# Layer 1's gating products traced ahead of the state-space mixer's last input product, and norms without GpSimd, in a two-layer hybrid block

## The chip, the cores and the metric

The kernel runs on one core of a Trainium2 chip. The metric is the device time of one execution in microseconds (us), the median of three runs. The engines are TensorE (PE, matmuls; PEld is its weight load), VectorE (DVE), ScalarE (ACT), GpSimd (POOL) and SyncE (SP, which issues the DMAs here). The granted clock of a row is TensorE's, as a share of 2.4 GHz; its lower level is 1.2 GHz.

## The reference, cut to what matters

Two layers over 512 latent tokens and 256 context tokens, width 1024. Each layer is: norm and modulation, one input projection for four mixers, output projection, norm and gated residual; then norm and modulation, gated feed-forward, norm and gated residual.

```python
def rmsnorm(x, g):
    return x * lax.rsqrt(jnp.mean(x * x, axis=-1, keepdims=True) + EPS) * g
for l in range(DEPTH):
    hx = rmsnorm(x, g_pre_mix[l]) * (1.0 + sc1x) + sh1x        # hc: the same of ctx
    in_x = jnp.split(hx @ w_in[l], SPLITS, axis=-1)             # four mixers' columns
    oa_x = chunk_mlp(in_x[0], ...)          # A: gelu; u * (spatial gate of v)
    ob_c, ob_x = gla_mixer(in_c[1], in_x[1], ...)   # B: gated linear attention
    oc_c, oc_x = s5_mixer(in_c[2], in_x[2], ...)    # C: state-space scan, both directions
    od_c, od_x = mla_mixer(in_c[3], in_x[3], ...)   # D: latent attention
    mix_x = jnp.concatenate([oa_x, ob_x, oc_x, od_x], axis=-1) @ w_out[l]
    x = x + gt1x * rmsnorm(mix_x, g_post_mix[l])
    hx = rmsnorm(x, g_pre_ffn[l]) * (1.0 + sc2x) + sh2x
    x = x + gt2x * rmsnorm(conv_ffn(hx, ...), g_post_ffn[l])
    if l < DEPTH - 1: ...                    # the same for ctx
return x
```

## The kernel before

Features lie on partitions and tokens along the free dimension. The tokens are three groups of 256: groups 0 and 1 are the latent tokens, group 2 is the context. Every fp32 weight is split into a high part (ACT, L191, `whi`) and a low part (DVE, L192, `wlo`), and so is every normed activation (`hh`/`hl`, for groups 0 and 1 together `hhx`/`hlx`); a product is three matmuls (L199 to L201) for each of eight blocks of the contraction. All DMAs go through SP's queue. The order of the instructions on each engine is chosen by the language's scheduler, which takes the order of the program text as priority; each engine then works through its own list in order. The program text is arranged by hand: the layers follow one another, and in the feed-forward `weave` mixes products ("units") with the steps of the norms ("chains") by scripts.

A norm of a group has a post-norm and, before a mixer or a feed-forward, a pre-norm. `sums` squares on ACT (L308), adds on DVE (L311) and sums over partitions on PE (L322); `rstd` takes the power on GpSimd (L125) and spreads it over the partitions on PE (L145), in PSUM. `post_norm` multiplies y by it and by the gate, and adds to x (L415 to L420). `modulate` scales and shifts x and splits it (L384 to L391). Of the eight blocks of 128 features, five go over DVE with the PSUM operand and three over GpSimd, which takes a copy in SBUF (L339).

At the boundary of the layers, group 0's, 1's and 2's post-norms and modulations follow one another. Mixer C's input products of layer 1 (`c_units`, ACT's copy L1218 into `rawm`) are units of layer 0's feed-forward, group after group; the last two, of group 2, come when group 2 is modulated. Then `mixers` opens its own PSUM pools and traces:

- `mixer_c`: transposes of `rawm` (L686), copies, second transposes (L693), B-products (L704), copies into the state `s5v` on DVE and ACT (L712, L714), then the scan on DVE: seven wide steps and eleven narrow ones (L725 to L728), and its wide closing passes (L743 to L753). The state is copied to `s5a` (L764, L766), multiplied out (L776, L778), goes through a gelu (L782), is transposed back (L788) and multiplied by the GLU's weights (L804 to L808), and is stored to `dmixr`.
- the other input products, in PSUM tiles `pg`: mixer A's u (`ua`, two products of 24 matmuls of 128x512) and v (`va`, 96 of 128x256, tokens on partitions), and mixer A (L980 to L995); then B's gates (products L835; ACT L838 to L842; DVE's subtraction L845, scan L846, L848 to L850), D's queries and keys and their norms (L1029 to L1044), B's q and k (L864, L869).

## Time and profile before

| | before |
|---|---|
| median of 3 runs | 1911.69 us (1909.13 to 1919.33) |
| the profiled execution | 1913.68 us |
| its span, from first to last instruction | 1911.9 us |
| mean granted clock of TensorE | 0.943 |

The span and what lies around it (1.8 us) make the profiled execution's time. All durations of the trace come from that one execution.

### The profile page before, as it was taken

Reading aid. Unit: us, or ns where it says so; the run is one execution under the profiler, and the core shown is the slowest. Engines: PE = TensorE matmul, PEld = TensorE weight load, DVE = VectorE, ACT = ScalarE, POOL = GpSimd, SP = SyncE. Lnnn points to the kernel's source line nnn. Section 1 sums busy time; section 2 is a strip of 40 time slices with the busy share of each in tenths; the row PEclk is TensorE's granted clock in tenths of the full one; section 3 lists DMA queues with packets and bytes.
Section 4 is the critical chain, followed back from the end, with each engine's and each line's share of the span. In section 5 each row is a group of like instructions: output and inputs, shape, how many; then the busy total and the mean of one; then the engine's idle time right before and its main releaser. Section 6 shows DMA issues by size and latency. Waiting matters only on the chain.

```text
span 1911.9 us, 28200 instructions
## 1 busy us (share of the span) xinstructions
PE 1778.6 (93%) x11256; PEld 1515.5 (79%) x11256; DVE 1197.0 (63%) x2200; ACT 775.5 (41%) x1241; POOL 122.3 (6%) x142
## 2 busy tenths in 40 slices
PE   5899989899988899999999998997989999999997
PEld 2785777689967788888888887886768988888886
DVE  8866634654899754684774674683465665454545
ACT  3433454444653333332331344364344653333332
POOL 0000000000430000000000033000000320000002
PEclk7999998899999999999999987998789899999998
DMA  9457630005623343352443333322102623323241
GB/s 351 154 174 243 192 95 23 28 26 201 199 66 120 113 133 99 114 163 78 148 128 111 101 120 104 113 70 86 43 23 84 195 86 81 109 86 110 79 150 47
DMA packets 94386, 222.14 MB, mean 116 GB/s; under 512 B 10928, under 2 KB 41008, under 8 KB 93232
## 3 DMA queue, kind: packets, MB, share of 16 engines
q1 hardware_dynamic: 94256, 220.36, 37.1%
q8 instruction: 88, 1.44, 0.3%
q14 instruction: 42, 0.34, 0.1%
HBM read 193.35 MB, written 24.08 MB: 114 GB/s over the span
## 4 chain that ended last, share of the span: by engine, by line
PE 71%; DVE 12%; issue 9%; ACT 4%; DMA 2%; POOL 1%; SPq 1%; POOLq 0%; DVEq 0%; ACTq 0%
PE pf L199 16%; PE pf L200 16%; PE pf L201 16%; PE pg L199 3%; PE pg L201 3%; PE pg L200 3%; PE pb L243 1%; PE pd L1151 1%; DVE z L1205 1%; DVE wlo L192 1%; PE pn L322 1%; DVE nu L389 1%; DVE hlx L391 1%; PE pc L704 1%; DVE junk L236 1%
## 5 line engine op out<-in xcount | busy, mean ns | idle before, releaser
L192 DVE TENSOR_TENSOR wlo<-raw,whi 128x1024 fp32r<-128x1024 f32 (+1 forms) x215 | 252.4, 1174 | 306.2 <-ACT whi L191 303.4
L191 ACT ACTIVATE whi<-raw 128x1024 fp32r<-128x1024 f32 (+1 forms) x215 | 217.4, 1011 | 407.7 <-PE pf L200 346.4
L199 PE MATMUL pf<-hhx,whi 128*128 128x512 f32 (+1 forms) x1032 | 365.4, 360 | 13.8 <-DVE z L1205 4.8
L200 PE MATMUL pf<-hlx,whi 128*128 128x512 f32 (+1 forms) x1032 | 370.1, 360 | 5.6 <-DVE hlx L391 5.1
L201 PE MATMUL pf<-hhx,wlo 128*128 128x512 f32 (+1 forms) x1032 | 367.2, 357 | 0.3 <-DVE wlo L192 0.3
L199 PEld LDWEIGHTS pf<-hhx,whi 128*128 128x128 f32 x1032 | 200.1, 197 | 42.2 <-ACT hhx L390 6.2
L200 PEld LDWEIGHTS pf<-hlx,whi 128*128 128x128 f32 x1032 | 202.4, 196 | 34.0 <-DVE hlx L391 9.2
L201 PEld LDWEIGHTS pf<-hhx,wlo 128*128 128x128 f32 x1032 | 202.6, 196 | 26.1 <-DVE wlo L192 0.5
L199 PE MATMUL pf<-g,whi 128*128 128x512 f32 (+1 forms) x552 | 185.2, 341 | 5.4 <-DVE z L1205 2.8
L201 PE MATMUL pf<-g,wlo 128*128 128x512 f32 (+1 forms) x552 | 186.5, 340 | 0.8 <-DVE wlo L192 0.8
L200 PE MATMUL pf<-g,whi 128*128 128x512 f32 (+1 forms) x552 | 186.9, 340 | 0.0
L1205 DVE SCALAR_TENSOR_TENSOR z<-pf,cols,z 128x511 f32<-128x511 f32 (+1 forms) x264 | 168.0, 656 | 24.3 <-ACT z L1203 21.7
L200 PE MATMUL pf<-hl,whi 128*128 128x256 f32 x432 | 123.7, 287 | 1.4 <-DVE hl L391 1.4
L199 PE MATMUL pf<-hh,whi 128*128 128x256 f32 x432 | 121.6, 286 | 1.8 <-ACT hh L390 1.8
L201 PE MATMUL pf<-hh,wlo 128*128 128x256 f32 x432 | 122.9, 285 | 0.0
L199 PEld LDWEIGHTS pf<-g,whi 128*128 128x128 f32 x552 | 104.3, 191 | 19.3 <-issue 4.0
L201 PEld LDWEIGHTS pf<-g,wlo 128*128 128x128 f32 x552 | 105.3, 191 | 12.3 <-DVE wlo L192 1.0
L200 PEld LDWEIGHTS pf<-g,whi 128*128 128x128 f32 x552 | 105.2, 191 | 11.5 <-DVE g L1255 0.2
L1203 ACT ACTIVATE z<-pf,cols 128x512 f32<-128x512 f32 (+1 forms) x132 | 89.9, 694 | 34.5 <-PE pf L201 29.3
L1284 DVE TENSOR_TENSOR y<-y,pf 128x512 f32<-128x512 f32 (+1 forms) x88 | 44.2, 514 | 71.0 <-PE pf L201 70.7
L125 POOL TENSOR_TENSOR nroy<-nroy,mhalf 128x2 f32<-128x2 f32 x10 | 9.9, 994 | 1202.3 <-DVE nroy L124 894.8
L200 PEld LDWEIGHTS pf<-hl,whi 128*128 128x128 f32 x432 | 83.5, 193 | 3.8 <-DVE hl L391 2.2
(457 smaller groups left out, 3406.3 us busy)
## 6 DMA issues: line engine op xcount, KB each, us to landing
raw<-in_w SPq DMA_DIRECT2D x170, 512.0 KB, 3.6
rawm<-in_wmod SPq DMA_DIRECT2D x64, 512.0 KB, 4.1
raw<-in_w SPq DMA_DIRECT2D x48, 384.0 KB, 3.2
wm<-in_wmod SPq DMA_DIRECT2D x8, 1024.0 KB, 10.6
silu<-in_wmod SPq DMA_DIRECT2D x16, 512.0 KB, 5.4
dx<-g SPq DMA_DIRECT2D x32, 256.0 KB, 2.2
dG<-gt SPq DMA_DIRECT2D x16, 256.0 KB, 2.3
dE<-es SPq DMA_DIRECT2D x16, 256.0 KB, 2.6
```

Source lines behind the costliest of these rows:

```text
L191: nc.scalar.activation(hv, src, AF.Copy)
L192: nc.vector.tensor_tensor(lv, src, hv.bitcast(F32), op=ALU.subtract)
L199: self.nc.tensor.matmul(out, lh, rh, start=i == 0, stop=False)
L200: self.nc.tensor.matmul(out, lh, rl, start=False, stop=False)
L201: self.nc.tensor.matmul(out, ll, rh, start=False, stop=i == n - 1)
L236: self.nc.vector.scalar_tensor_tensor(junk[:], wt, 1.0, self.silu[w][:], op0=ALU.mult, op1=ALU.mult, accum_out=self.modacc[l][:, w, m:m + 1])
L243: self.nc.tensor.matmul(acc[32 * q:32 * q + 2, :], self.ct[:, k, :], halves[q // 2][:, q % 2 * 512:q % 2 * 512 + 512], start=k == 0, stop= ...
L322: self.nc.tensor.matmul(ps[:, j:j + 1], acc[:, k, j * 128:(j + 1) * 128], self.ones[:, 0:1], start=k == 0, stop=k == 1)
L389: nc.vector.scalar_tensor_tensor(u[:], xk, sc, pb, op0=ALU.mult, op1=ALU.mult)
L1203: nc.scalar.activation(z[:, o:o + m], p[:, :m], AF.Identity, bias=b, scale=w1)
L1205: self.last = nc.vector.scalar_tensor_tensor(z[:, o + d:o + d + m - 1], p[:, s:s + m - 1], w, z[:, o + d:o + d + m - 1], op0=ALU.mult, op1 ...
L1284: nc.vector.tensor_tensor(y[:, m, t0:t0 + tw], y[:, m, t0:t0 + tw], ps[:, :tw], op=ALU.add)
```

## The change

Two things are changed.

First, the units of group 2's input product of mixer C are no longer issued at the end of the feed-forward. Its PSUM pool stays open, and in layer 1 `mixers` traces in its banks (tag "pf") first va's product, then ua's, then the two late units; only then is the pool closed and are the mixers' pools opened. Since the late units come from a second call of `c_units`, their two weight halves are loaded and split a second time. In layer 0 mixer C is traced first as before; ua and va have changed places.

Second, GpSimd keeps only the power in the norms. After the squares ACT multiplies y by the gate in place; `post_norm` is then two DVE passes of 128x512 for each pair of blocks. `modulate` is, for each pair, one DVE product of 128x512, four ACT passes of 128x256 (scale and shift, once for the high part and once in full), and one DVE subtraction of 128x512.

```diff
@@ -333,16 +331,13 @@
     def feature_rstd(self, pool, psp, ptag, width, pv):
         return self.rstd(pool, self.sums(pool, psp, ptag, width, pv))
-    def pool_copy(self, pool, pb, x=""):
-
-        sb = self.t(pool, [128, 256], "npb" + x, bufs=1)
-        self.nc.scalar.copy(sb[:], pb)
-        return sb[:]
-
     def norms(self, l, part, g, yp, xp, pool, psp, store=None, pre=None):
         ps = self.sums(pool, psp, "pn", 512, yp, "o")
+        for k in range(KT):
+            yk = yp(k // 2)[:, k % 2, :]
+            self.nc.scalar.activation(yk, yk, AF.Copy, scale=self.modc(l, part, k, g))
         yield
         pb = self.rstd(pool, ps, "o")
         yield
@@ -370,26 +365,19 @@
             for _ in c:
                 pass
-    def modulate(self, l, part, g, pv, pool, pb, kdve=KDVE):
+    def modulate(self, l, part, g, pv, pool, pb):
         nc = self.nc
         self.new_h(g)
-        sb = self.pool_copy(pool, pb) if kdve < KT else None
-        for k in KORDER:
-            xk = pv(k // 2)[:, k % 2, :]
-            u = self.t(pool, [128, 256], "nu", bufs=3)
-            sh, sc = self.modc(l, part, k, g), self.modc(l, part + 1, k, g)
-            hh, hl = self.hh[g][:, k, :], self.hl[g][:, k, :]
-            if k >= kdve:
-                w = self.t(pool, [128, 256], "nw", bufs=2)
-                nc.gpsimd.tensor_tensor(u[:], xk, sb, op=ALU.mult)
-                nc.scalar.activation(hh, u[:], AF.Identity, bias=sh, scale=sc)
-                nc.scalar.activation(w[:], u[:], AF.Identity, bias=sh, scale=sc)
-                nc.gpsimd.tensor_tensor(hl, w[:], hh.bitcast(F32), op=ALU.subtract)
-            else:
-                nc.vector.scalar_tensor_tensor(u[:], xk, sc, pb, op0=ALU.mult, op1=ALU.mult)
-                nc.scalar.activation(hh, u[:], AF.Identity, bias=sh)
-                self.hlast = nc.vector.scalar_tensor_tensor(hl, u[:], sh, hh.bitcast(F32), op0=ALU.add,
-                                                            op1=ALU.subtract)
+        for i in range(KT // 2):
+            u = self.t(pool, [128, 2, 256], "nu", bufs=2)
+            nc.vector.tensor_tensor(u[:], pv(i), pb.unsqueeze(1).to_broadcast([128, 2, 256]), op=ALU.mult)
+            ks = slice(2 * i, 2 * i + 2)
+            w = self.t(pool, [128, 2, 256], "nw", bufs=2)
+            for k in (2 * i, 2 * i + 1):
+                sh, sc = self.modc(l, part, k, g), self.modc(l, part + 1, k, g)
+                nc.scalar.activation(self.hh[g][:, k, :], u[:, k % 2], AF.Identity, bias=sh, scale=sc)
+                nc.scalar.activation(w[:, k % 2], u[:, k % 2], AF.Identity, bias=sh, scale=sc)
+            self.hlast = nc.vector.tensor_tensor(self.hl[g][:, ks], w[:], self.hh[g][:, ks].bitcast(F32), op=ALU.subtract)
     def new_hx(self):
@@ -404,23 +392,14 @@
     def post_norm(self, l, part, g, yp, xp, pool, pb, squares):
-        acc, seen = None, set()
+        acc = None
         nc = self.nc
-        sb = self.pool_copy(pool, pb, "o")
-        for k in KORDER:
-            yk, xk = yp(k // 2)[:, k % 2, :], xp(k // 2)[:, k % 2, :]
-            u = self.t(pool, [128, 256], "nuo", bufs=2)
-            gate = self.modc(l, part, k, g)
-            if k >= KDVE:
-                nc.gpsimd.tensor_tensor(u[:], yk, sb, op=ALU.mult)
-                nc.scalar.activation(u[:], u[:], AF.Copy, scale=gate)
-                nc.gpsimd.tensor_tensor(xk, xk, u[:], op=ALU.add)
-            else:
-                nc.vector.scalar_tensor_tensor(u[:], yk, gate, pb, op0=ALU.mult, op1=ALU.mult)
-                nc.vector.tensor_tensor(xk, xk, u[:], op=ALU.add)
-            seen.add(k)
-            if squares and k ^ 1 in seen:
-                acc = self.square(pool, acc, xp(k // 2))
+        for i in range(KT // 2):
+            y, x = yp(i), xp(i)
+            nc.vector.tensor_tensor(y, y, pb.unsqueeze(1).to_broadcast([128, 2, 256]), op=ALU.mult)
+            nc.vector.tensor_tensor(x, x, y, op=ALU.add)
+            if squares:
+                acc = self.square(pool, acc, x)
         return acc
@@ -1379,8 +1358,13 @@
             ctx = l < L - 1
             G = (0, 1, 2) if ctx else (0, 1)
             tn = T if ctx else NX
-            self.mixers(l, ctx, md, (psls, tabs, tables) if l == 0 else None)
-            with self.pool("f") as fp, self.pool("psf", space=PSUM) as psp:
+            if l == 0:
+                self.mixers(l, ctx, md, early=(psls, tabs, tables))
+            else:
+                self.mixers(l, ctx, md, late=(psf, psp, late))
+            psf = self.pool("psf", space=PSUM)
+            psp = psf.__enter__()
+            with self.pool("f") as fp:
                 with self.pool("y1") as yp:
                     y = self.t(yp, [128, KT, T], "y")
                     def out_units(groups):
@@ -1488,17 +1472,18 @@
                     if ctx:
                         uf = [self.t(self.wp, [128, D], "rawm", bufs=2)[:, :T] for _ in range(2)]
                         self.uf[l + 1] = uf
-                        cu, late = self.c_units(l + 1, uf, psp)
+                        cu = self.c_units(l + 1, uf, psp)[0]
+                        late = self.c_units(l + 1, uf, psp)[1]
                         self.weave(WV[4], down[1], c[:1])
                         self.weave(WV[5], down[2] + cu[:2], c[:2])
                         self.weave(WV[6], cu[2:], c[1:])
-                        self.weave("", late, [])
                     else:
                         self.weave(WV[7], down[1], c)
             xsrc = xd
+        psf.__exit__(None, None, None)
         es.close()
-    def mixers(self, l, ctx, md, early=None):
+    def mixers(self, l, ctx, md, early=None, late=None):
         nc = self.nc
         G = (0, 1, 2) if ctx else (0, 1)
         G3 = (0, 1, 2)
@@ -1541,16 +1526,46 @@
         def store(o, k, mix, t0=0):
             nc.sync.dma_start(md[:, o + k, t0:tn], mix[:, t0:tn])
+        rest = iter(())
+
+        def visit(n):
+            for _ in range(n):
+                next(rest, None)
+
+        mxs = self.pool("mx")
+        px_ = mxs.__enter__()
+        env = SimpleNamespace()
+        x12 = self.t(px_, [128, 4, T], "x12")
+        x6 = self.t(px_, [128, 1536], "x6")
+        ut = x12[:, 0:2]
+        va = x12[:, 2:4].rearrange("p a t -> p (a t)").rearrange("p (i c) -> p i c", i=6)
+
+        def va_product():
+            tmajor("va", G, lambda g, ps: nc.scalar.activation(
+                va[:, 2 * g:2 * g + 2].rearrange("p i c -> p (i c)"), ps[:], AF.Gelu_apprx_tanh))
+
+        def ua_product():
+            for i in range(2):
+                px, pc = fm(half("ua", i), G)
+                evac(ut[:, i], px, pc, func=AF.Gelu_apprx_tanh)
+                visit(1)
+
+        if late:
+
+            psf, psp, units = late
+            self.psg = psp, "pf"
+            va_product()
+            ua_product()
+            for u in units:
+                u()
+            psf.__exit__(None, None, None)
         psls, tabs, tables = early or (self.pool("psb", space=PSUM), None, None)
         if not early:
             self.psp = psls.__enter__()
         pcs = self.pool("pcp", space=PSUM, side="right")
         pcp = pcs.__enter__()
         psgs = self.pool("psg", space=PSUM)
-        self.psg = psgs.__enter__()
-        mxs = self.pool("mx")
-        px_ = mxs.__enter__()
-        env = SimpleNamespace()
+        self.psg = psgs.__enter__(), "pg"
         def heads(n, x, groups):
             w = 256 * len(groups)
@@ -1575,16 +1584,9 @@
             if l == 0:
                 rest = chain(*(self.mod_pair(p, self.gate) for p in (1, 2)))
             visit(2)
-            x12 = self.t(px_, [128, 4, T], "x12")
-            x6 = self.t(px_, [128, 1536], "x6")
-            ut = x12[:, 0:2]
-            va = x12[:, 2:4].rearrange("p a t -> p (a t)").rearrange("p (i c) -> p i c", i=6)
-            for i in range(2):
-                px, pc = fm(half("ua", i), G)
-                evac(ut[:, i], px, pc, func=AF.Gelu_apprx_tanh)
-                visit(1)
-            tmajor("va", G, lambda g, ps: nc.scalar.activation(
-                va[:, 2 * g:2 * g + 2].rearrange("p i c -> p (i c)"), ps[:], AF.Gelu_apprx_tanh))
+            if not late:
+                ua_product()
+                va_product()
             visit(2)
             self.mixer_a(l, ut, va, x6, px_, "pb2", ctx)
             visit(2)
```

What the scheduler makes of it on PE, at the boundary. The names: `pf` and `pg` are products, `pn` norm sums (L322, now L320) and broadcast (L145, now L143), `pc` mixer C's tiles. Before: the end of group 2's product, the first transposes, ua's two products (pg_11117, pg_11149), va's first (pg_11187), the first B-product.

```order
L200 MATMUL pf_10698<-hl_1561_10631,whi_10433 128x256
...
L201 MATMUL pf_10698<-hh_1560_10630,wlo_10434 128x256
L686 MATMUL pc_1585_10774<-cst_68,rawm_9983 96x128
L686 MATMUL pc_1585_10774<-cst_68,rawm_9984 96x128
...
L199 MATMUL pg_11117<-hhx_3557,whi_11113 128x512
L200 MATMUL pg_11117<-hlx_3558,whi_11113 128x512
L201 MATMUL pg_11117<-hhx_3557,wlo_11114 128x512
...
L686 MATMUL pc_1587_10786<-cst_68,rawm_9983 96x128
...
L199 MATMUL pg_11149<-hhx_3557,whi_11145 128x512
...
L199 MATMUL pg_11187<-whi_11177,hhx_3557 128x256
...
L704 MATMUL pc_1594_10823<-s5u_10798,s5e_10749 128x96 x4
```

Now: pf_10570 and pf_10620 are va's two tiles, pf_10676 and pf_10708 ua's, pf_10740 and pf_10772 group 2's; pf_10453 is the last of group 1's. The first fence runs from group 1's product to the start of group 2's.

```order
L197 MATMUL pf_10570<-whi_10560,hhx_3557 128x256
...
L199 MATMUL pf_10453<-hhx_3557,wlo_10337 128x256
L320 MATMUL pn_10502<-ones_70,nsa_10481 128x1 x4
L197 MATMUL pf_10570<-whi_10566,hhx_3557 128x256
L197 MATMUL pf_10620<-whi_10566,hhx_3557 128x256
L197 MATMUL pf_10676<-hhx_3557,whi_10672 128x512
...
L143 MATMUL pn_10502<-cst_68,nry_10507 128x128 x2
L199 MATMUL pf_10570<-whi_10560,hlx_3558 128x256
...
L198 MATMUL pf_10620<-wlo_10567,hhx_3557 128x256
...
L199 MATMUL pf_10676<-hhx_3557,wlo_10673 128x512
...
L197 MATMUL pf_10708<-hhx_3557,whi_10704 128x512
...
L197 MATMUL pf_10740<-hh_1486_10512,whi_10736 128x256
```

The second goes on from group 2's last row; L665 is the first transpose (before: L686), pg_11214 is a product of the latent queries, L970 is mixer A's spatial product.

```order
L199 MATMUL pf_10772<-hh_1486_10512,wlo_10769 128x256
L665 MATMUL pc_1531_10838<-cst_68,rawm_9920 96x128
L665 MATMUL pc_1531_10838<-cst_68,rawm_9921 96x128
...
L197 MATMUL pg_11214<-hhx_3557,whi_11210 128x512
L198 MATMUL pg_11214<-hlx_3558,whi_11210 128x512
L199 MATMUL pg_11214<-hhx_3557,wlo_11211 128x512
...
L970 MATMUL pb_1575_11184<-x_1499_10557,x_1498_10556 64x128 x2
L665 MATMUL pc_1533_10850<-cst_68,rawm_9920 96x128
```

All of ua and va has moved from between the transposes and B-products to places ahead of the first transpose: 24 rows of va among group 1's product, 26 rows of both between group 2's sums and its broadcast, 94 behind the broadcast; the 48 of group 2 follow. Between the transposes stand the latents' products now.

On DVE, at the end of layer 1's scan. Before: s5v and s5a rows are the scan's, L753 128x11x96 is its last; bg and bsc are B's gates.

```order
L192 TENSOR_TENSOR wlo_11827<-raw_11824,whi_11826 128x1024
L846 SCALAR_TENSOR_TENSOR bg_11478<-brs_11475,bsc_11479 128x768
L728 TENSOR_TENSOR s5v_10747<-s5v_10747,s5a_10899 128x32
L846 SCALAR_TENSOR_TENSOR bg_11478<-brs_11475,bsc_11479 128x768
...
L750 TENSOR_TENSOR s5v_10747<-s5v_10747,s5a_10899 128x11x128
...
L752 TENSOR_TENSOR s5a_10899<-s5l_10753,s5v_10747 128x1408
L753 TENSOR_TENSOR s5v_10747<-s5v_10747,s5a_10899 128x11x128
...
L752 TENSOR_TENSOR s5a_10899<-s5l_10753,s5v_10747 128x1056
L192 TENSOR_TENSOR wlo_12304<-raw_12301,whi_12303 128x1024
L753 TENSOR_TENSOR s5v_10747<-s5v_10747,s5a_10899 128x11x96
L845 TENSOR_TENSOR bsc_11479<-bsc_11479,bg_11478 128x768 x2
...
L846 SCALAR_TENSOR_TENSOR bg_11478<-brs_11475,bsc_11479 128x768 x2
```

Now (L704 was L725, L729 to L732 were L750 to L753; L1012 are the latents' sums, L843 scales B's q, L1023 scales the latents by their norms):

```order
L1012 TENSOR_SCALAR dms_11437<-pb_1601_11417 128x4
L704 TENSOR_TENSOR s5a_10963<-s5l_10817,s5v_10811 128x64
...
L843 SCALAR_TENSOR_TENSOR x_1608_11460<-x_1608_11460,bsc_11531 128x512
L704 TENSOR_TENSOR s5a_10963<-s5l_10817,s5v_10811 128x64
...
L1023 SCALAR_TENSOR_TENSOR ck_10552<-ck_10552,cols_9_80,pb_1606_11445 96x768
L729 TENSOR_TENSOR s5v_10811<-s5v_10811,s5a_10963 128x11x128
L731 TENSOR_TENSOR s5a_10963<-s5l_10817,s5v_10811 128x1408
L1023 SCALAR_TENSOR_TENSOR cq_10551<-cq_10551,cols_9_80,pb_1607_11453 128x512
L1023 SCALAR_TENSOR_TENSOR cq_10551<-cq_10551,cols_9_80,pb_1607_11453 96x512
L732 TENSOR_TENSOR s5v_10811<-s5v_10811,s5a_10963 128x11x128
...
L731 TENSOR_TENSOR s5a_10963<-s5l_10817,s5v_10811 128x1056
L732 TENSOR_TENSOR s5v_10811<-s5v_10811,s5a_10963 128x11x96
```

The gates' second half (two scans, before behind the scan's last pass), the scaling of B's q and that of the latents have moved ahead of the scan's last passes. In all, between the scan's first and last row there are now four gate scans for two, four passes of each kind of the gates' subtractions for two (the first product pass three for four), four of L843, three of L1023, and five splits for seven; mixer A's five passes stand ahead of the scan.

## Rows read from the trace of the kernel before

**Rows 1.** Busy us, share of the span and instructions of an engine, whole span.

```profile
PE 1778.6 (93%) x11256; PEld 1515.5 (79%) x11256; DVE 1197.0 (63%) x2200; ACT 775.5 (41%) x1241; POOL 122.3 (6%) x142
```

**Rows 2.** Windows: bounds, length, busy of PE, PEld, DVE, ACT, POOL, granted clock, DMA.

```profile
1130.00:1150.00 20.00, 16.69 (x77) 14.58 (x77) 15.02 (x31) 11.89 (x27) 11.44 (x16) 0.59 0.15 52
1150.00:1170.00 20.00, 15.15 (x66) 12.97 (x65) 13.59 (x25) 9.66 (x21) 11.10 (x16) 0.59 0.25 76
...
1216.00:1260.00 44.00, 44.00 (x246) 35.69 (x246) 34.94 (x68) 18.52 (x24) 1.83 (x1) 1.00 0.32 95
1260.00:1284.00 24.00, 22.41 (x155) 20.23 (x154) 23.78 (x27) 12.53 (x14) 0.00 (x0) 1.00 0.23 71
1284.00:1324.00 40.00, 30.36 (x164) 26.98 (x164) 19.27 (x35) 22.96 (x33) 2.26 (x1) 0.74 0.23 65
```

**Rows 3.** PE's timeline at the boundary: start, duration, line, operands [idle before].

```profile
1143.22 1.02 PE L322 MATMUL pn<-ones,nsa 128*128 128x1 f32 x8 [0.20 <-DVE nsa L311]
...
1162.23 1.37 PE L322 MATMUL pn<-ones,nsa 128*128 128x1 f32 x8 [1.57 <-DVE nsa L311]
1164.72 1.22 PE L145 MATMUL pn<-cst,nry 128*128 128x128 f32 x4 [1.12 <-POOL nry L125]
...
1178.51 1.00 PE L686 MATMUL pc<-cst,rawm 128*96 128x128 f32 x7 [0.87 <-ACT rawm L1218]
```

**Rows 4.** Groups by line, 1120 to 1178: busy, mean ns, idle before.

```profile
L417 POOL TENSOR_TENSOR g<-g,nuo 128x256 f32<-128x256 f32 x6 | 5.2, 869 | 1.4 <-ACT nuo L416 1.4
...
L390 ACT ACTIVATE hhx<-nu,mod 128x256 fp32r<-128x256 f32 x10 | 5.0, 498 | 0.4 <-DVE nu L389 0.4
```

**Rows 5.** Groups by line and shape, whole span.

```profile
L1284 DVE TENSOR_TENSOR y<-y,pf 128x512 f32<-128x512 f32 x32 | 21.9, 686 | 49.2 <-PE pf L201 49.1
```

**Rows 6.** Timeline of POOL and of DVE in the norms after layer 0's mixers.

```profile
515.78 1.83 POOL L417 TENSOR_TENSOR g<-g,nuo 128x256 f32<-128x256 f32 x1 [1.33 <-ACT nuo L416]
...
510.32 1.77 DVE L192 TENSOR_TENSOR wlo<-raw,whi 128x1024 fp32r<-128x1024 f32 x1
```

**Rows 7.** PE's timeline, two matmuls of ua and two of va in a row.

```profile
1188.73 0.39 PE L199 MATMUL pg<-hhx,whi 128*128 128x512 f32 x1
1188.95 0.39 PE L200 MATMUL pg<-hlx,whi 128*128 128x512 f32 x1
...
1207.60 0.28 PE L200 MATMUL pg<-wlo,hhx 128*128 128x256 f32 x1
1207.72 0.28 PE L201 MATMUL pg<-whi,hlx 128*128 128x256 f32 x1
```

**Rows 8.** DVE's timeline: the scan's first pass, a wait inside, its last pass.

```profile
1216.65 0.96 DVE L725 TENSOR_TENSOR s5a<-s5l,s5v 128x768 f32<-128x768 f32 x1 [1.79 <-ACT s5v L714]
...
1255.43 0.96 DVE L845 TENSOR_TENSOR bsc<-bsc,bg 128x768 f32<-128x768 f32 x1 [2.80 <-ACT bg L842]
...
1280.29 1.25 DVE L753 TENSOR_TENSOR s5v<-s5v,s5a 128x1056 f32<-128x1056 f32 x1
```

**Rows 9.** DVE's groups by line and shape, 1178 to 1284.

```profile
L192 DVE TENSOR_TENSOR wlo<-raw,whi 128x1024 fp32r<-128x1024 f32 x13 | 15.9, 1222 | 21.9 <-ACT whi L191 21.9
...
L845 DVE TENSOR_TENSOR bsc<-bsc,bg 128x768 f32<-128x768 f32 x4 | 3.7, 953 | 2.8 <-ACT bg L842 2.8
L846 DVE TENSOR_TENSOR_SCAN bg<-brs,bsc 128x768 f32<-128x768 f32 x2 | 3.5, 1750 | 0.0
```

**Rows 10.** The chain that ended last, in order of time: start, duration, what.

```profile
1310.21 1.28 ACT L863
...
1311.50 1.15 ACT bsc L863 x2
...
1318.02 1.71 PE pb L145 x8
...
1327.38 4.99 DMA bk<-bk
```

More of the change, by code (lines that the diff above doesn't have):

```diff
@@ L29 @@
 NCH = T // 8
-KDVE = 5
 PB = 3
-XK, RK, KS = 4, 7, KT
+XK, RK = 4, 7
 AHD = 0
@@ L35 @@
 WV = ["uu0u0u00u0", "0u0u0u0u", "0u0u0u0u", "", "0uu0u0uu0u0", "1u0u1u0u1uu1u", "0101u0u0u0", "0u0u0u0u"]
-KORDER = [0, 5, 1, 2, 6, 3, 4, 7]
 TAB0 = 2
@@ L1362, in chain @@
                 yield
-                self.modulate(0, 0, g, xv, sp, pb, KS)
+                self.modulate(0, 0, g, xv, sp, pb)
             c = [chain(g) for g in range(3)]
@@ L1513, in fm @@
             if 0 in groups:
-                px = self.t(self.psg, [128, 512], "pg")
+                px = self.t(self.psg[0], [128, 512], self.psg[1])
                 self.gemm_fm(wv, KT, self.hrhs, px, None, [g for g in groups if g < 2])
             if 2 in groups:
-                pc = self.t(self.psg, [128, 512], "pg")
+                pc = self.t(self.psg[0], [128, 512], self.psg[1])
                 self.gemm_fm(wv, KT, self.hrhs, None, pc[:, :256], [2])
@@ L1532, in tmajor @@
             for g in groups:
-                ps = self.t(self.psg, [128, 512], "pg")
+                ps = self.t(self.psg[0], [128, 512], self.psg[1])
                 for j in range(2):
@@ L1562, in heads @@
                     nc.sync.dma_start(x[64 - hr * 64:128 - hr * 64, 2 * hp + hr, :w], x[rs, 2 * hp + hr, :w])
-        rest = iter(())
-        def visit(n):
-            for _ in range(n):
-                next(rest, None)
         with self.pool("mc") as pm:
```

## The prediction

> **What bounds the kernel now.** I read the busy shares first: TensorE (PE) is busy for 1778.6 of 1911.9 us, VectorE (DVE) for 1197.0 [rows 1]. An average like that says little about a change at one place, so I read the windows around the layer boundary and through layer 1's mixers. Three regimes stand there [rows 2]. From 1130 to 1170, while the last post-norms run, PE is busy for 31.84 of 40 us at a granted clock of 0.59, so most of that stretch is at the 1.2 GHz level. From 1216 to 1260 PE is busy without a gap at full clock, while DVE works 34.94 of 44 us. From 1260 to 1284 DVE is busy for 23.78 of 24 us, and afterwards, from 1284 to 1324, PE falls to 30.36 of 40 at a clock of 0.74. The chain of work passes through the same places: the state-space scan's last steps on DVE, ScalarE's (ACT) gelu, the short products behind it, then the store of the result and the exchange of k at 1327.38 [rows 10]. So from 1260 to 1330 the state-space mixer sets the end, and PE with all its other products waits for it. How early its transposes start, how long its scan takes on DVE with what is queued between its steps, and how long its tail is: these three decide.
>
> **The move, first term: when the state-space mixer starts.** In the kernel before, group 2's sums start at 1162.23, their broadcast at 1164.72 for 1.22 (so it ends 3.7 after the sums began), then PE does 48 products for group 2, and the transposes run from 1178.51 [rows 3]. The gating products (ua: 48 of 128x512, va: 96 of 128x256) are fillers behind it, between transposes and B-products. Now PE's row lists put them ahead, but not where PE idles: 24 of va lie among group 1's products, 26 rows between group 2's sums and its broadcast, and everything else behind the broadcast and ahead of the first transpose. PE works in order, so the transposes wait for all of it.
>
> When do group 2's sums come? From group 1's sums at 1143.22 [rows 3] its broadcast ends 3.7 later, at 1146.9. Then DVE has, for one modulate and one post-norm, 8 + 8 passes of 128x512 and 3 additions of squares. The nearest row is the addition from PSUM of that size, 0.686 [rows 5]; 19 of these are 13.0, and because starts overlap a little I take 12. ACT has 16 passes for the modulate at 0.50 [rows 4], 8.0, with 8 gates and 4 squares beside or behind, so it ends at 12 to 14 too. Sums at 1159, 3 earlier than now (from 1156, if the stage gains all that GpSimd's 0.87 passes [rows 4] cost, to 1162). The 26 rows cost 24 x 0.12 + 2 x 0.23 = 3.3 by the steps between starts [rows 7], nearly hidden in the 2.5 from sums to broadcast; the broadcast ends at 1163.5. Behind it: 48 of va at 0.12 (5.8), 46 of ua at 0.23 (10.6), 48 for group 2 at 0.12 (5.8), together 22.2, then some 1.2 for the evacuation, as now. Transposes from 1187 against 1178.5: **+8.4** (from +5, with the sums at 1156, to +11, with the sums at 1162 or the first 3 of the 22 us at the lower clock).
>
> **Second term: fillers inside the mixer.** PE fills the gaps between transposes and B-products with what comes next. Before: 48 x 0.23 + 96 x 0.12 + 11 x 0.23 = 25.0. Now the queries', keys' and latents' products, 79 x 0.23 + 48 x 0.12 = 23.9, and mixer A's spatial products and one gate product, which came later before: some 16 to 40 rows of which I have no group here, between 16 steps of 0.12 and 20 of 0.23, 2 to 5, and I take 4. **+3** (1 to 4). The scan's first step, at 1216.65 now [rows 8], starts at 1228.
>
> **Third term: the scan on DVE.** It runs from 1216.65 to 1281.5, 64.9 us [rows 8]. DVE's list shows what stands between its first and last step. New there: two gate scans at 1.75, two subtractions at 0.95 and four passes alike, and seven scalings of about 128x512 at 0.69: 3.5 + 1.9 + 3.8 + 4.8 = 14.0, and some 1 of small copies. Gone ahead of it: two weight splits at 1.22, one gate pass, and mixer A's five passes: 2.4 + 0.95 + 1.2 + 2.8 = 7.4 [rows 5, 9]. Net +7.6. DVE's idle in the stretch was 44 - 34.94 + 24 - 23.78 = 9.3 [rows 2]; one wait of 2.80 for ACT's gate functions is the largest [rows 8]. Those functions wait for gate products behind the fillers; relative to the scan these now come earlier, so I take 2 off. **+5.6** (0, if all waits go, to +10).
>
> **Fourth term: the tail.** What was done earlier is missing behind the scan: ACT's table load 1.28 and 1.15 of the gate functions, and the norm's broadcast of 1.71 between the last short products [rows 10]; **-4.5** (-6 to 0). From there the exchange of k waits for the same instructions as before, so the rest shifts one to one. Mixer: 8.4 + 3 + 5.6 - 4.5 = +12.5.
>
> **Layer 0's mixers and the second weight load.** In layer 0 the order stays state-space first and PE has no gap there; nothing. The second load and split of group 2's two weight halves is two splits on DVE and two on ACT in a stretch where each has 5 or more of 20 us free [rows 2]; hidden unless PE catches up with it, then up to 1.2 each.
>
> **Norms elsewhere.** There are four more places: the start, after layer 0's mixers, after layer 1's, and the end. DVE loses the passes of 128x256 in favour of fewer of 128x512; ACT has 16 passes per modulate where it had 11, so that where a modulate runs alone it takes 16 x 0.50 = 8 instead of some 7. One us at the start, up to 2 after layer 0's mixers, about -1 at the end, where GpSimd's chain ended last: together **+1** (-5 to +5).
>
> The trace shows GpSimd and DVE disturbing each other: a GpSimd addition took 1.83 and a split on DVE, at the same stretch, 1.77, against 0.87 and 1.22 in the means [rows 4, 6, 9]. The Trainium skill (SBUF — State Buffer, Who interferes with whom) says that a DVE instruction with two SBUF inputs and a GpSimd instruction that reads SBUF exclude each other for a whole instruction. By it every split and addition beside a norm gets shorter; the trace agrees for the pairs above. That is the second rival's mechanism.
>
> **Sum.** 12.5 + 1 = 13.5 on the profiled execution's 1913.68 gives 1927.2; that execution was 2.0 over the median of 1911.69, so **1925** for the median.
>
> **Rivals.** *The gaps take the products (faster).* In 1130 to 1170, 31.84 us at 0.59 would be 18.8 at full clock, so 21 of 40 are to be had. If the 22 us of ua and va lay in there and kept the clock up, the transposes would start 2 to 3 earlier than now, the scan would begin as now or earlier without its 9.3 of waits (7.6 - 9.3 = -1.7), the tail gives 4.5 and the norms 4: some -12, **1899**. It decides from the point where more than half of the products run before group 2's sums. For it: PE's idle and clock at the boundary. Against it: in the list only 24 + 26 of 144 stand there. The Trainium skill (TensorE: Matmul & The Clock Gate, HAM oscillation — how this bites in real kernels) says that waits between groups of matmuls bring the slower clock back, and that a loop that keeps PE fed avoids it; the 0.59 agrees, and by that rule the time would be this rival's. Chance 0.20.
>
> *Contention and gates cancel (no change).* If the boundary's norm stage shortens by all that GpSimd cost, 6 instead of 3, the other norms by 4, and the scan has no waits left, the terms are 5 + 3 + 0 - 5 - 4 = -1: **1911**. For it: POOL is busy 22.5 of these 40 us. Against it: ACT takes over what GpSimd leaves and has its own 8 us per modulate. Chance 0.18.
>
> *PE stalls at the closing of the PSUM pool (slower).* The mixers' banks are taken from the feed-forward's only when its last tile is evacuated; if va's gelu queues behind ACT's modulates, PE waits for its bank in front of ua, 3 to 5 more: **1930**. Chance 0.07.
>
> **How the numbers follow.** My forecast, a later and longer scan, has 0.55, by itself 1912 to 1938. A measurement of this kernel can tell about 0.5%, 9.6 us, from no change: faster is below 1902.1, slower above 1921.3. Of my forecast's 0.55 I count 0.42 as slower and 0.13 as same; the first rival gives 0.17 faster and 0.03 same; the second 0.14 same and 0.04 faster; the third 0.07 slower. Faster 0.21, same 0.30, slower 0.49. The range from 1900 to 1940 leaves out most of the first rival (0.12) and about 0.05 above.
>
> **What the profile after would show.** Right: group 2's sums at 1156 to 1162; a PE without gaps from there; the transposes' first row near 1187; the scan's first step at 1225 to 1231 and its end near 1298; a PE that idles between about 1250 and the end of the scan, since its products are done; no GpSimd passes except the power. Wrong: transposes before 1180 (the gaps took the products), a scan below 62 us (its waits went and the rest didn't come in), or an end of the mixer that moves without the end of the kernel.

## The result, and the profile after

The changed kernel takes 1942.43 us, median of four runs (1936.8 to 1945.3), where the kernel before has 1915.51 over four: 1.0133 of it, with a 95% interval of 1.0111 to 1.0156, some 25 us slower. The forecast of slower was right, the size of +13.5 was not: the time lies above the range. Of the 17.4 us between 1942.43 and the forecast of 1925, 3.8 are the kernel before itself, whose median is 1911.69 over the three runs that the forecast started from and 1915.51 with a fourth. The profiled execution, the fastest of the four, has 1936.80 us and a span of 1935.0, 23.1 longer than before.

The engines' busy times of the page after (as [rows 1]):

```profile
PE 1776.7 (92%) x11256; PEld 1514.4 (78%) x11256; DVE 1188.8 (61%) x2142; ACT 825.7 (43%) x1339; POOL 31.1 (2%) x34
```

PE does the same work. GpSimd has lost 91 us, ACT has gained 50, and DVE, which took over GpSimd's blocks, is not busier: its passes are twice as wide and fewer (their prices are in the last section). The windows at the boundary and through layer 1's mixers (columns as in [rows 2]):

```profile
1130.00:1150.00 20.00, 14.41 (x93) 13.29 (x93) 17.06 (x30) 16.62 (x33) 1.39 (x2) 0.74 0.37 116
1150.00:1170.00 20.00, 18.58 (x113) 17.36 (x113) 13.79 (x25) 13.46 (x26) 2.67 (x5) 0.74 0.17 57
...
1260.00:1280.00 20.00, 16.67 (x108) 14.49 (x106) 18.65 (x25) 11.75 (x11) 0.00 (x0) 1.00 0.19 49
1280.00:1310.00 30.00, 11.30 (x48) 10.54 (x48) 26.14 (x61) 6.35 (x11) 2.27 (x1) 0.54 0.09 28
1310.00:1345.00 35.00, 21.95 (x116) 17.99 (x116) 5.47 (x12) 16.09 (x23) 0.00 (x0) 0.76 0.22 61
```

PE now runs out of products: from 1280 to 1310 it works 11.30 of 30 us, at a granted clock of 0.54, so mostly at the 1.2 GHz level, while DVE is busy for 26.14 with the scan and the passes queued between its steps. PE's timeline (as [rows 3]) has the sums and the broadcast of group 2, the first seven transposes (L665, before: L686), and two of its waits:

```profile
1167.64 0.95 PE L320 MATMUL pn<-ones,nsa 128*128 128x1 f32 x8
...
1172.65 0.60 PE L143 MATMUL pn<-cst,nry 128*128 128x128 f32 x4
...
1196.51 1.00 PE L665 MATMUL pc<-cst,rawm 128*96 128x128 f32 x7 [1.18 <-ACT rawm L1197]
...
1283.88 0.37 PE L1008 MATMUL pb<-ones,bsc 96*128 96x1 f32 x1 [6.42 <-ACT bsc L1006]
...
1313.09 1.17 PE L757 MATMUL pc<-s5e,s5a 128*96 128x128 f32 x4 [12.40 <-ACT s5a L745]
```

DVE's timeline (as [rows 8]): the scan's first pass, a wait for the gates, a wait for the latents' sums on PE, the scan's last pass.

```profile
1237.39 0.96 DVE L704 TENSOR_TENSOR s5a<-s5l,s5v 128x768 f32<-128x768 f32 x1 [2.92 <-ACT s5v L693]
...
1248.26 0.96 DVE L824 TENSOR_TENSOR bsc<-bsc,bg 128x768 f32<-128x768 f32 x1 [2.20 <-ACT bg L821]
...
1290.99 0.16 DVE L1012 TENSOR_SCALAR dms<-pb 128x4 f32<-128x4 f32 x1 [2.76 <-PE pb L1008]
...
1308.58 1.26 DVE L732 TENSOR_TENSOR s5v<-s5v,s5a 128x1056 f32<-128x1056 f32 x1
```

Where the 23.1 us come in is seen by setting the starts of the same instructions beside each other. The table gives how much later than before each stands, in us of the profiled executions; e1, e2, e4, e5 and e9 are experiments of the next section. The first seven transposes are 18.0 later (1196.51 for 1178.51 in [rows 3]), the last eight, in the table, 16.2.

| start of | before | after | e1 | e2 | e4 | e5 | e9 |
|---|---|---|---|---|---|---|---|
| layer 0's first transposes | 74.61 | +3.7 | -0.6 | +4.2 | +0.3 | -0.5 | -1.8 |
| last down products of layer 0, first row | 1097.49 | +8.0 | 0.0 | +7.4 | -1.5 | +4.1 | +5.2 |
| layer 1's last transposes | 1185.55 | +16.2 | +10.0 | +1.6 | -8.1 | +14.1 | -6.8 |
| the scan's first pass | 1216.65 | +20.7 | +13.3 | +1.7 | -7.9 | +17.5 | -16.3 |
| the scan's last pass | 1280.29 | +28.3 | +17.8 | +1.7 | -7.9 | +21.9 | -32.9 |
| mixer C's last pass | 1323.60 | +20.8 | +11.6 | -1.6 | -9.8 | +14.3 | -21.1 |
| layer 1's second norm, first product of group 1 | 1524.63 | +18.5 | +10.9 | -1.9 | -10.9 | +15.2 | -11.5 |
| the same, last product | 1554.21 | +22.8 | +11.5 | +2.0 | -11.5 | +16.3 | -11.4 |

One execution wanders: e5 and e9 come out of layer 0's mixers 5 to 6 later than e4, where nothing of theirs differs from e4, and e7, which is as before up to the boundary, is 5.4 late there. The windows show a different granted clock in the same stretch, first in the kernel before (0.95), then in e7 (0.80), then in the changed kernel (0.85):

```profile
235.00:270.00 35.00, 33.41 (x207) 28.99 (x206) 15.78 (x30) 21.64 (x31) 2.27 (x1) 0.95 0.26 80
```

```profile
235.00:270.00 35.00, 33.61 (x188) 29.64 (x186) 13.85 (x28) 21.53 (x31) 2.27 (x1) 0.80 0.14 44
```

```profile
235.00:270.00 35.00, 34.84 (x219) 31.57 (x218) 16.71 (x31) 19.62 (x26) 2.27 (x1) 0.85 0.23 69
```

So a lag of 8.0 at the boundary need not all come from the norms. Steps inside a stage are read from the table, totals from the medians.

### The profile page after: what moved, and what is told of

Same layout as the page of the kernel before. It is cut to its first block, busy times and chain, and to the rows that moved or that the text cites. A ratio compares the mean times of both kernels' runs of the same rounds, so it can differ in the third digit from the quotient of the medians.

```text
span 1935.0 us, 28082 instructions
## 1 busy us (share of the span) xinstructions
PE 1776.7 (92%) x11256; PEld 1514.4 (78%) x11256; DVE 1188.8 (61%) x2142; ACT 825.7 (43%) x1339; POOL 31.1 (2%) x34
## 4 chain that ended last, share of the span: by engine, by line
PE 75%; DVE 13%; ACT 6%; issue 3%; DMA 3%; SPq 0%; POOL 0%; DVEq 0%; POOLq 0%; ACTq 0%
PE pf L197 17%; PE pf L198 17%; PE pf L199 17%; PE pg L197 3%; PE pg L199 3%; PE pg L198 3%; PE pd L1130 2%; PE pb L241 1%; DVE wlo L190 1%; ACT nw L379 1%; DVE z L1184 1%; PE pd L1123 1%; PE pb L891 1%; ACT hhx L378 1%; PE pc L757 1%
## 5 line engine op out<-in xcount | busy, mean ns | idle before, releaser
L197 PE MATMUL pf<-hhx,whi 128*128 128x512 f32 (+1 forms) x1048 | 375.9, 360 | 15.7 <-DVE z L1184 9.6
L198 PE MATMUL pf<-hlx,whi 128*128 128x512 f32 (+1 forms) x1048 | 375.2, 358 | 9.1 <-DVE hlx L380 9.1
L199 PE MATMUL pf<-hhx,wlo 128*128 128x512 f32 (+1 forms) x1048 | 373.6, 357 | 0.5 <-DVE wlo L190 0.5
L197 PEld LDWEIGHTS pf<-hhx,whi 128*128 128x128 f32 x1048 | 204.8, 196 | 43.9 <-issue 9.7
L197 PEld LDWEIGHTS pf<-hh,whi 128*128 128x128 f32 x432 | 82.2, 191 | 2.9 <-ACT hh L378 1.0
```

Source lines behind the costliest of these rows:

```text
L197: self.nc.tensor.matmul(out, lh, rh, start=i == 0, stop=False)
L198: self.nc.tensor.matmul(out, lh, rl, start=False, stop=False)
L199: self.nc.tensor.matmul(out, ll, rh, start=False, stop=i == n - 1)
```

## The experiments

All ratios are to the kernel before, with 95% intervals, over 6 to 12 runs each.

**e1, the move alone**: the changed kernel with `norms`, `modulate` and `post_norm` of before.

```diff
-                self.modulate(0, 0, g, xv, sp, pb)
+                self.modulate(0, 0, g, xv, sp, pb, KS)
...
```

> The kernel before with the move alone (gating products and late units in the feed-forward's banks), norms as before. Theory (the move costs some 12 us in layer 1's mixers and nothing elsewhere, the norms the rest): 1.006 of before, 8 to 16 us longer, up to the layer boundary within 2 us of before, the first seven transposes at about 1188, the scan's end near 1300. Rival (the move is harmless, group 2's late norm stage did it): within 4 us of before.

Measured: 1.0081 (1.0055 to 1.0106), 15.5 us. Up to the boundary nothing changes, the seven transposes start at 1190.70, the scan's last pass stands at 1298.1. The theory holds, the rival falls.

**e2, the norms alone**: the kernel before with those three functions of the changed one; seen from the changed kernel:

```diff
-                self.mixers(l, ctx, md, late=(psf, psp, late))
+            self.mixers(l, ctx, md, (psls, tabs, tables) if l == 0 else None)
...
+                        self.weave("", late, [])
```

> The kernel before with the norms of the change alone, products in their old places. Theory: the norms cost some 11 us in all, 3 to 4 at the start, 3 after layer 0's mixers, 3 after layer 1's, and give back about 3 at the boundary: 1.004 to 1.006 of before. Rival (norms are neutral by themselves, as the forecast had it, and what was lost ahead of the boundary is this one execution's clock): within 5 us of before.

Measured: 1.0029 (1.0013 to 1.0046), 5.5 us. It is less than the theory's 11, but by the table not as the rival has it: 4.2 are lost at the start and 7.4 by the boundary (the wander in layer 0's mixers included), 3.9 in layer 1's second norm, and 6 are given back at the boundary, twice what was expected.

**e3, the new post-norm alone**, with the modulate of before:

```diff
+            self.nc.scalar.activation(yk, yk, AF.Copy, scale=self.modc(l, part, k, g))
...
+            nc.vector.tensor_tensor(y, y, pb.unsqueeze(1).to_broadcast([128, 2, 256]), op=ALU.mult)
+            nc.vector.tensor_tensor(x, x, y, op=ALU.add)
```

> The kernel before with the new post-norm alone (gate on ScalarE, pairs on VectorE); modulate keeps its five and three blocks. Theory (the modulate's second ScalarE pass is what costs): no longer than before, 0 to 8 us shorter. Rival (the gate in the post-norm costs): 4 to 8 us longer.

Measured: 1.0017 (0.9996 to 1.0038). Neither a gain nor a clear loss: it decides nothing.

**e4, no GpSimd and one ScalarE pass**: e2 with this modulate.

```diff
-                nc.scalar.activation(self.hh[g][:, k, :], u[:, k % 2], AF.Identity, bias=sh, scale=sc)
-                nc.scalar.activation(w[:, k % 2], u[:, k % 2], AF.Identity, bias=sh, scale=sc)
...
+        for k in range(KT):
...
+            nc.vector.scalar_tensor_tensor(u[:], xk, sc, pb, op0=ALU.mult, op1=ALU.mult)
+            nc.scalar.activation(hh, u[:], AF.Identity, bias=sh)
+            nc.vector.scalar_tensor_tensor(hl, u[:], sh, hh.bitcast(F32), op0=ALU.add, op1=ALU.subtract)
```

> The kernel before with the new post-norm and with a modulate that has all eight blocks on VectorE in the old form, one ScalarE pass each; GpSimd has the power alone. Theory (the second ScalarE pass costs): the start as before to 0.5 us, in all within 4 us of before and 6 to 10 shorter than with the norms of the change. Rival (taking GpSimd away costs by itself, whatever the form): as long as with the norms of the change, within 3 us.

Measured: 0.9956 (0.9934 to 0.9977), 8 us faster than before and 14 faster than e2. The mechanism is the theory's and the gain larger than it said; the start is back to +0.3. The second pass is seen in ACT's timeline of the changed kernel at the start, where the modulates of two groups run on without a gap from 57.74 to 74.1, and in DVE's, where subtractions wait for it:

```profile
57.74 0.60 ACT L378 ACTIVATE hhx<-nu,mod 128x256 fp32r<-128x256 f32 x1 [3.46 <-DVE nu L373]
58.24 0.59 ACT L379 ACTIVATE nw<-nu,mod 128x256 f32<-128x256 f32 x1
...
65.13 0.59 ACT L379 ACTIVATE nw<-nu,mod 128x256 f32<-128x256 f32 x1
65.62 0.59 ACT L378 ACTIVATE hh<-nu,mod 128x256 fp32r<-128x256 f32 x1
...
73.54 0.60 ACT L379 ACTIVATE nw<-nu,mod 128x256 f32<-128x256 f32 x1
```

```profile
65.75 0.69 DVE L380 TENSOR_TENSOR hlx<-nw,hhx 128x512 fp32r<-128x512 f32 x1 [0.68 <-ACT nw L379]
...
74.17 0.69 DVE L380 TENSOR_TENSOR hl<-nw,hh 128x512 fp32r<-128x512 f32 x1 [1.28 <-ACT nw L379]
```

Over the whole kernel 28 of the 44 subtractions wait for that second pass, 24.5 us in all, in the changed kernel; DVE's subtractions in the kernel before have ten such waits for ACT, 3.0 us. First the changed kernel, then the kernel before: who waited for whom, us in total, times, longest.

```profile
DVE hlx L380 <- ACT nw L379: 13.6, 17, 1.5
DVE hl L380 <- ACT nw L379: 10.9, 11, 1.8
```

```profile
DVE hlx L391 <- ACT hhx L390: 1.8, 6, 0.5
DVE hl L391 <- ACT hh L390: 1.2, 4, 0.5
```

In e4 it is 0.9 in five. e4 also undoes the modulate's pairs of 128x512; no run keeps the pairs and drops the second pass, so the two go together in what follows.

The windows of the start, first of the changed kernel, then of e4, show ACT's load: 31.21 of 38 us against 18.77 of 35.

```profile
41.00:79.00 38.00, 27.18 (x172) 24.93 (x173) 26.76 (x62) 31.21 (x62) 0.00 (x0) 0.81 0.35 129
```

```profile
40.00:75.00 35.00, 27.73 (x169) 25.85 (x170) 28.95 (x82) 18.77 (x39) 0.00 (x0) 0.78 0.42 154
```

**e5, the move with e4's norms**: the changed kernel with e4's modulate.

> The changed kernel with the modulate in the old form on VectorE for all eight blocks, one ScalarE pass each; move and new post-norm as in the change. Theory (the modulate's second ScalarE pass costs some 12 us over the kernel, the move 11, and the shorter norm stage at the boundary is lost where the move makes TensorE the bound there): start as before to 0.5 us, 9 to 13 shorter than the changed kernel, so 1.004 to 1.008 of before, and 15 to 19 longer than e4. Rival (the effects only add): 11 longer than e4, 1.001 to 1.002 of before.

Measured: 1.0064 (1.0041 to 1.0087): 13 us shorter than the changed kernel, as expected, and 21 longer than e4, a little more than expected. So the modulate with the second pass costs 13 to 14 us with the move or without it (0.0069, 0.0073), and the move 20 with new norms (e5 over e4, changed kernel over e2) and 15.5 with old ones. The rival's figures give less than e5's interval; but they took 11 for the move, and with the 15.5 that e1 measured, adding gives 1.0037, so near that the medians don't exclude it. For the theory speak the steps of the table from the last down products to the last transposes: the new norms shorten them by 5.8 (e2) and 6.6 (e4) without the move, with the move by 1.8 (changed kernel over e1) and 0.0 (e5). What the faster norm stage gains at the boundary is lost there, where the move has put PE's work behind it.

**e6, va alone ahead** (on e1):

```diff
             va_product()
-            ua_product()
             for u in units:
...
-            if not late:
-                ua_product()
+            ua_product()
+            if not late:
                 va_product()
```

> The move with va's product alone ahead of group 2's; ua's product stays in the mixers, norms as before. Theory (the products that stand between group 2's norm and the transposes delay the scan one for one): 48 rows of ua at 0.23, 11 us, less ahead; transposes within 2 us of before instead of 10 later, the whole 4 to 7 longer than before or less. Rival (the scan on VectorE and the gates between its steps cost, not its start): as long as the whole move, 10 or more over before.

Measured: 1.0059 (1.0039 to 1.0079), 11 us; the intervals of e6 and e1 overlap. The transposes are within 2 us of before, as the theory said, and yet it gained nothing sure: the last sixteen B-products and the scan's first pass stand 9.0 later, since the scheduler fills the gaps between transposes and B-products with as many later products. From the last transposes to these B-products it takes 35.4, against 27.8 in the kernel before. PE's timeline of e6, then of the kernel before, where the transposes start at 1185.55:

```profile
1186.92 0.27 PE L686 MATMUL pc<-cst,rawm 128*96 128x128 f32 x1
...
1222.34 1.92 PE L704 MATMUL pc<-s5u,s5e 128*128 128x96 f32 x16
```

```profile
1213.36 1.03 PE L704 MATMUL pc<-s5u,s5e 128*128 128x96 f32 x8
```

The theory was too narrow: what counts is all of PE's work ahead of the last B-product, not what stands ahead of the transposes.

**e7, group 2's units ahead of va and ua, weights kept** (on e1):

```diff
-                        cu = self.c_units(l + 1, uf, psp)[0]
-                        late = self.c_units(l + 1, uf, psp)[1]
+                        cu, late = self.c_units(l + 1, uf, psp)
...
-            va_product()
-            ua_product()
             for u in units:
                 u()
+            va_product()
+            ua_product()
```

> The whole move with group 2's units traced ahead of va and ua, and their weights kept from the first call (no second load and split); norms as before. Theory (the transposes wait for the feed-forward's PSUM pool to close, whatever the order in it): transposes 10 to 14 later than before, in all as long as the whole move or up to 4 longer. Rival (group 2's product being last, or the second load and split, is what delays): transposes within 4 us of before.

Measured: 1.0117 (1.0093 to 1.0141), 22 us, 7 longer than e1. The last transposes are 21.6 late, of which 5.4 were there before the boundary: 16, more than expected, as is the total. The order among the products and the second load and split are not what delays. ACT's row and PE's row of e7 show what stands between: the last of group 2's products is copied into `rawm` by 1183.03, and the transposes start at 1202.25, behind the last row of ua and without a wait of PE. In the program the mixers' PSUM pools open behind the feed-forward's closing, so what uses its banks comes ahead of the transposes in PE's list, as the theory has it.

```profile
1182.67 0.36 ACT L1218 COPY rawm<-pf 128x256 f32<-128x256 f32 x1
...
1202.25 1.03 PE L686 MATMUL pc<-cst,rawm 128*96 128x128 f32 x8
```

**e8, GpSimd's blocks to DVE in the old form**, on the kernel before:

```diff
-KDVE = 5
+KDVE = KT
```

> The kernel before with KDVE at eight: no block of a norm on GpSimd, every pass of VectorE as before in 128x256. Theory (GpSimd's three blocks gain nothing, and the pairs of the new post-norm are what makes e4 faster): within 4 us of before, 5 to 10 longer than e4. Rival (the removal of GpSimd from the norms is the gain by itself): as fast as e4 within 3 us.

Measured: 1.0030 (1.0012 to 1.0048), 6 us over before, somewhat more than the theory's 4, and 14 over e4. Removing GpSimd gains nothing by itself, nor does the new post-norm by itself (e3); e4 has both.

**e9, the scan first**: e4, and in layer 1 every input product of the other mixers is held behind the last B-product.

```diff
+                        self.cgate = nc.tensor.matmul(ps[:, g * NCH:(g + 1) * NCH], E..., U[:, gg, :], ...)
...
+                with self.behind(self.cgate if l else None):
                     self.gemm_fm(wv, KT, self.hrhs, px, None, [g for g in groups if g < 2])
...
```

> e4 with layer 1's input products of the other mixers held behind the last B-product of the state-space mixer, so that TensorE runs transposes and B-products with nothing between them (25 us of ua and va before). Theory (how early the scan starts sets the end of the mixers): scan's first step 10 to 14 us earlier than in e4, its stretch some us longer or shorter, and 4 to 10 us off the whole, 0.990 to 0.994 of before. Rival (TensorE's sum of products sets it, so that its idle time there, some 8 us at a lower clock, is lost): 4 to 10 us longer than e4.

Measured: 0.9903 (0.9877 to 0.9929), 18 us faster than before and 10 faster than e4. DVE's timeline of e9, then of e4, with the scan's first and last pass:

```profile
1200.39 0.96 DVE L705 TENSOR_TENSOR s5a<-s5l,s5v 128x768 f32<-128x768 f32 x1 [8.34 <-ACT s5v L694]
...
1247.44 1.26 DVE L733 TENSOR_TENSOR s5v<-s5v,s5a 128x1056 f32<-128x1056 f32 x1
```

```profile
1208.80 0.96 DVE L705 TENSOR_TENSOR s5a<-s5l,s5v 128x768 f32<-128x768 f32 x1 [1.84 <-ACT s5v L694]
...
1272.39 1.25 DVE L733 TENSOR_TENSOR s5v<-s5v,s5a 128x1056 f32<-128x1056 f32 x1
```

The scan starts 8.4 earlier (15 relative to the boundary, which this execution of e9 reached 6.7 later) and takes 48.3 us instead of 64.8, because the gates' products, held back too, reach DVE only afterwards: e4 has 14.3 us of gate passes between the scan's first and last step, e9 none. So of the 24.9 us by which the scan ends earlier, 16.5 come from its length. The end gains less than the scan, since PE is now the bound to the end of the mixers: 64.00 of 64 us in this window of e9. The profiled executions hide the gain (spans of 1900.3 and 1900.6): e9's is the slowest of its six, e4's the fastest of its eight.

```profile
1200.00:1264.00 64.00, 64.00 (x386) 55.01 (x385) 51.25 (x89) 25.01 (x35) 2.90 (x1) 1.00 0.30 89
```

**e10**: the same, held behind the second transposes (L693) only.

```diff
+                self.cgate = nc.tensor.transpose(ps[:, g * NCH:(g + 1) * NCH], uc[:NCH, g0 + g]...,
...
-                        self.cgate = nc.tensor.matmul(ps[:, g * NCH:(g + 1) * NCH], E..., U[:, gg, :], ...)
+                        nc.tensor.matmul(ps[:, g * NCH:(g + 1) * NCH], E..., U[:, gg, :], ...)
```

> As e9, but the products are held behind the last of the second transposes only, so that they fill between the B-products. Theory (scan's start): 3 to 7 us earlier start than in e4, and 2 to 6 off the whole, between e4 and e9. Rival (sum of products): 0 to 5 longer than e4.

Measured: 0.9938 (0.9914 to 0.9962), 12 us faster than before. It lies between e4 and e9 as the theory has it, but its interval overlaps both. The scan starts 6.1 earlier than in e4 (1202.75) and is hardly shorter (63.6 us), since gate passes stand in it again.

**e11**: e9's hold in both layers.

```diff
-                with self.behind(self.cgate if l else None):
+                with self.behind(self.cgate):
...
```

> As e9, with the other mixers' products held behind the last B-product in layer 0 as well. In layer 0 TensorE has no gap from 80 to 260 in the kernel before. Theory (where TensorE's sum of products bounds, an earlier scan gives nothing and the gap is lost): 3 to 10 us longer than e9, lost between layer 0's first transposes and its feed-forward. Rival (the scan's start sets the end of the mixers in both layers): 4 to 10 us shorter than e9.

Measured: 1.0075 (1.0053 to 1.0097), 33 us longer than e9. The sign is the theory's, the size far over it: in layer 0 the B-products wait for tables that the kernel builds at that time, so PE stands still for them. From 80 to 260 it works 148.87 of 180 us, where the kernel before has 179.38; two of the waits in PE's timeline of e11:

```profile
100.47 0.93 PE L684 MATMUL pc<-s5u,s5e 128*128 128x96 f32 x3 [6.67 <-DVE gt L615]
...
135.16 1.14 PE L684 MATMUL pc<-s5u,s5e 128*128 128x96 f32 x4 [9.15 <-DMA s5e<-dE]
```

**e12**: e9's hold in the kernel before, its norms unchanged.

> The kernel before, norms and all, with layer 1's products held behind the last B-product as in e9. Theory (the scan's start in layer 1 is worth 6 to 11 us whatever the norms): 0.993 to 0.997 of before. Rival (it is worth something only with e4's shorter norm stage): within 4 us of before.

Measured: 0.9957 (0.9938 to 0.9976), 8 us faster than before; the hold is worth it with the old norms too.

## Why the prediction was wrong, step by step

**The mixers: right in mechanism and sum, with errors in the terms that cancel.** Group 2's sums stand at 1167.64, 1159.6 without the 8.0 that were already lost at the boundary; predicted 1159. The first term, +8.4, measured +10.0 (1196.51 less 8.0, against 1178.51). The second, +3, measured +2.7 (18.0 at the first seven transposes, 20.7 at the scan's first pass). The third, +5.6, measured +7.6 (20.7 to 28.3): the work came in as priced (7.6; DVE's busy time in the stretch rose from 56.26 to 64.03), but the 2 us of waits that were to go stayed. The fourth, -4.5, measured -7.5 (28.3 to 20.8). Together +12.8 against +12.5; that it is so near is in part luck, and by the medians the move costs 15.5 (e1). PE's predicted idle time up to the end of the scan is there. e9 and e12 show that an earlier and shorter scan ends the mixers earlier; what its start alone is worth is not shown, since in both the gates leave the scan as well, and e10, which moves the start and leaves the gates, gains 3.5 over e4 within the noise. The second weight load costs nothing that e7 could show.

**The step that failed: "Norms elsewhere", +1 with -5 to +5.** By the medians it is 10 us (the changed kernel over e1). In the trace 3.7 come in at the start for a predicted 1, 4.3 in layer 1's second norm, for which the sum had nothing, and 0.3 at the end for a predicted -1. The norms after layer 0's mixers take 71.4 from their first sums to their last, 69.7 before: 1.7, for a predicted "up to 2". Together 10.0. What else is lost by the boundary (8.0 less 3.7 and 1.7) lies in stages where executions with the same norms differ by as much.

Two things were wrong in the working. It counted 11 ACT passes in every modulate before, and that is not so at the start: there `modulate` is called with `KS`, which is eight, so all eight blocks went over DVE, not five, and ACT had 8 passes, 0.40 apart where they follow one another (the row below, of the kernel before, has three in 1.31), some 3 us. Now it has 16, 0.49 apart, 7.9 us; the forecast put this at one us more.

```profile
53.99 1.31 ACT L390 ACTIVATE hhx<-nu,mod 128x256 fp32r<-128x256 f32 x3 [2.36 <-DVE nu L389]
```

And it set the modulate's 8 us against "some 7" as if each modulate stood alone. They follow one another, two without a gap of ACT at the start, elsewhere with squares, gates and copies between, and DVE's subtraction, for which PE's next product waits (13.8 us over the kernel, 8.9 before), waits for ACT. e2 against e4, and the changed kernel against e5, put 13 to 14 us on the modulate's new form; the waits for `nw` point to its second pass.

**The rivals.** *The gaps take the products*: the clock at the boundary rose to 0.74 and PE works 32.99 of 40 us there from 1130 to 1170, for 31.84 before, but the transposes came later all the same; e6 and e7, which place them otherwise, are no faster than before either. The Trainium skill (TensorE: Matmul & The Clock Gate, HAM oscillation — how this bites in real kernels) says that waits between groups of matmuls bring the slower clock; the trace agrees where PE waits for the scan, at 0.54 from 1280 to 1310. *Contention and gates cancel*: e8 takes GpSimd out and gains nothing; single passes do get longer beside GpSimd [rows 6], but whether that was hidden or is made up for by the blocks that DVE takes over is not shown. The rival's gain in the norms, 5 and 4 us, is what e4 gets (8) with one ACT pass in the modulate. *PE stalls at the pool's closing*: no such wait stands in PE's timeline; the 1.18 at 1196.51 is for `rawm`. The pool's closing costs by the order that it gives (e7), and that was in the first term.

**What stays open**: e3 does not tell what the gate on ACT costs by itself; the modulate's second pass and its pairs were not tried apart, nor the scan's start and the gates within it; and the median of e1 (15.5) is 4 above its profiled execution (11.2, the fastest of six), which one trace can't resolve.

## What to carry to other kernels

An engine that takes over work "beside" the others is priced in the stage where somebody waits for it, for all groups in a row, not by its busy share: ACT's 41% hid a stage in which DVE's subtractions came to wait for it. Count its passes at each call, too: a parameter made the start unlike the other places. Where one serial chain sets the end (here a scan on DVE), count all of PE's work that stands ahead of its last input; moving one product away lets the scheduler put another there, and holding the others back by an explicit order was worth 8 to 10 us. The same hold loses 33 us where the chain's inputs are themselves late, so look first at what the chain's start waits for.

## What the runs showed of the hardware that was not expected

A DVE product with the PSUM broadcast costs 682 ns for 128x512, where two of 128x256 with the gate cost 948 (474 each). The post-norm's addition in SBUF, the same operation in both, costs 686 for 128x512 and 836 for two of 128x256 (418 each), so the width alone takes 150 ns off a pair there; in the product the width is not told apart from the gate's move to ACT. Such narrow passes fit the 14 us by which e8 is longer than e4, but the two kernels also differ in the order of the blocks and in ACT's copy of the broadcast that e8 still makes (ten of 0.37 us), and e3, with the same post-norm and the modulate of before, gains nothing. The changed kernel's groups, then e8's, by line and shape from 1120 to 1190:

```profile
L400 DVE TENSOR_TENSOR g<-g,y 128x512 f32<-128x512 f32 x12 | 7.8, 686 | 0.0
L399 DVE TENSOR_TENSOR y<-y,pn 128x512 f32<-128x512 f32 x11 | 6.8, 682 | 0.0
```

```profile
L419 DVE SCALAR_TENSOR_TENSOR nuo<-y,mod,pn 128x256 f32<-128x256 f32 x20 | 8.8, 474 | 0.0
L420 DVE TENSOR_TENSOR g<-g,nuo 128x256 f32<-128x256 f32 x20 | 8.0, 418 | 0.0
```
